# Column and row groups in turn for the small matmuls of the mixers, and y of the RWKV scan kept by chunk with a pair of heads on the partitions

## The chip, the cores and the metric

The kernel runs on one core of a Trainium2 chip. The metric is the time of one execution in device microseconds (us). Everything is fp32; the large products split an operand into a high and a low part and are run as fp32r matmuls, the small ones of the mixers run as fp32.

## What is computed

The reference is one layer of a streaming encoder for 2048 prompt rows and 32 sample rows of 1024 channels. Each row is normalised, projected (`W_in`), sent through four mixers of 256 output channels each, projected back (`W_out`) and added to the residual; a gated feed-forward part follows. The change touches two mixers, B (the RWKV scan) and D (attention). Cut to that:

```
# mixer B, 4 heads of 64; lat_w, lat_a are 32 wide, lat_g is 64 wide
w_log  = -softplus(-(w0 + tanh(lat_w) @ w2)) - 0.5
a_rate = sigmoid(a0 + lat_a @ a2)
gate   = sigmoid(lat_g) @ g2
for each row t, each head:                      # wkv7_step
    sa = S @ a_t
    S  = S * w_t + sa b_t^T + v_t k_t^T
    y  = S @ r_t
y = (y - mean(y)) * rsqrt(var(y) + GN_EPS)      # over the 64 values of a head
y = (y * gn_g + gn_b + bonus) * gate
# mixer D: 4 query heads, 2 key/value heads, window of 128 rows back, whole chunks of 64
p = softmax(q k^T with mask and sink);  o = p v
```

## The kernel before

Three stages follow one another: the mixers with both projections (0 to about 1110 us), the feed-forward gate and up products, and the down projection. In the mixers the prompt runs in eight blocks of 256 rows, each of two tiles of 128 rows, and the sample rows go along with one of the blocks. The code of a block is written as steps named by the letters of `ORD` (L67): scan, projection, attention and so on of this block, the input projection of the next one and the output projection of the one before. A scheduler then orders all instructions of an engine by priorities (a `high_priority` offset on some steps) and by when it thinks an operand is there, so PE's row of small matmuls is filled up with matmuls of the projections (`pj`, `pjd` for the input, `po` for the output, all in `mm3`, L93 to L95). PE executes its row strictly in that order.

PSUM has 8 banks: three for the projections ("mm"), one "nx", two "rk" for the scan and its preparation, two "at" for attention and the low-rank products. The tiles of a tag take turns in its banks; a new tile waits until every reader of the old one is done.

The names in what follows:

- **Scan** (`scan`, in `rwkv`): a tile of 128 rows is worked in two chunks of 64 rows. A chunk computes `wp` from the state `stp` and `aup` (L884), adds a part that is ready (`ww`, L886), makes the state's update `pp` (L891) and the new state on VectorE (L895), and the output `yp`. Of `yp`, rows 64c to 64c+63 are the chunk's 64 rows, and its columns are (pair of heads, head of the pair, value). So all matmuls of a chunk's `yp` write the same 64 PSUM partitions: the state's part `stp`,`arp` (L897, all 128 rows of the array, 64 columns), then per head `wwp`,`trp` (L901) and `vtokp`,`krp` (L902), 64 rows by 64 columns. Which 64 columns of the array a matmul takes follows from the PSUM partitions it writes; which 64 rows, from the partitions that it reads. `pp` writes its two heads of a pair to different 64 partitions, one after the other.
- **Statistics**: once per tile, on all 128 rows: four `bn_stats` and `bn_aggr` (L908, L909), a reciprocal square root (`rsqrt`: a VectorE instruction L117 and a power on GpSimd L118, tile `grsp`), one VectorE instruction for the shift (L911), four ScalarE instructions that write the normalised y, `gynp` (L913). `rwkv_out` transposes `gynp` by pair of heads (L1001) and applies the channel's scale and shift.
- **Attention** (`attn`): for each key/value head `kv` two score matmuls `asp` (L675) that read partitions 64kv to 64kv+63, the softmax, transposes `aptp` into `apt` (L710, L711), and two matmuls `aot` (L713; one in the first tile) that write partitions 64kv to 64kv+63, from the previous and this tile's values `avt`. `apt` has one buffer, so the second head's copy waits for the first head's `aot`.
- **Low-rank products** (`rwkv_prep`, L741): `pw`, `pa`, `pg`, two matmuls each, reading partitions 0 to 31, 32 to 63, 64 to 127 of `lap`; all in the "at" banks.
- **Weights**: in the first block `load_unit` reads `W_in` tile by tile into `wraw` (SyncE, L390), ScalarE makes the high part (L380) and GpSimd, or VectorE for a few, the low part (L382) of `whl`, which is also stored for the later blocks. `wraw` and the residual tiles `xr` of the output projection (L1084) share `XRB` = 6 buffers of 128x256.

Of the kernel before, what the change touches and what calls it, by code (L numbers as in the profile page):

```python
# [8 lines left out]
F32 = mybir.dt.float32  # L9
# [11 lines left out]
GN_EPS = 64e-5  # L21
# [11 lines left out]
def layer(tc, ins, outs):  # L33
# [13 lines left out]
    NB = SEQ // TB  # L47
    SB = 1 if NB > 1 else 0
    ctx = ExitStack()
    XRB = 6  # L50
    PWP = 3000
    RSD = 1
    EVP = 3000
# [594 lines left out]
    def attn(sg, b, i, r, yh, yl):  # L648
        n, PT = sg.name, sg.PT
        samp = sg is seg_s  # L650
        qkv, qn = r["qkv"][i], r["qns"][i]
        gi = b * seg_p.NT + i
        st = b4.tile([128, 12], F32, tag="ast2", name="ast2", bufs=1)
        tp = px([128, 3, 128], "atp", "at")
        for g in range(2):
            TE.transpose(tp[:, g, :PT], qn[:PT, 2 * g:2 * g + 2, :].rearrange("p h d -> p (h d)"), ident[:PT, :PT])
        TE.transpose(tp[:, 2, :PT], qn[:PT, 4:6, :].rearrange("p h d -> p (h d)"), ident[:PT, :PT])
        qt = b4.tile([128, 2, 128], F32, tag="aqt", name="aqt", bufs=1)
        S.activation(qt[:, :, :PT], tp[:, 0:2, :PT], AF.Copy, scale=gq8[:, 0:1])
        if samp:  # L660
            ktr, k0, c0, NK = kt_s, 128, 0, 128 + PT
        else:
            if i == 0:
                if gi:
                    S.activation(ktb[:, 0:128], ktb[:, TB:TB + 128], AF.Copy)
            ktr, k0 = ktb, 128 + i * 128
            c0 = k0 - 128 if gi else k0
            NK = k0 + 128 - c0
        V.tensor_scalar(ktr[:, k0:k0 + PT], tp[:, 2, :PT], P("gk"), None, op0=MUL)
        pr = b4.tile([128, 4, 256], F32, tag="apr", name="apr", bufs=1)  # L670
        for kv in range(2):
            sp = px([128, 2, 256], "asp", "at")
            o = slice(64 * kv, 64 * kv + 64)
            for g in range(2):
                TE.matmul(sp[:PT, g, :NK], qt[o, g, :PT], ktr[o, c0:c0 + NK], start=True, stop=True)  # L675
            if samp:
                V.tensor_copy(pr[:PT, 2 * kv:2 * kv + 2, :NK], sp[:PT, :, :NK])
            else:
                V.tensor_tensor(pr[:PT, 2 * kv:2 * kv + 2, :NK].rearrange("p g (a k) -> p g a k", k=64),
                                sp[:PT, :, :NK].rearrange("p g (a k) -> p g a k", k=64),  # L680
                                amask[:, 4 - NK // 64:].unsqueeze(1).unsqueeze(3).to_broadcast([128, 2, NK // 64, 64]), op=ADD)
        V.tensor_reduce(st[:PT, 0:4], pr[:PT, :, :NK], axis=AX.X, op=MAX)
        V.tensor_tensor(st[:PT, 0:4], st[:PT, 0:4], sinks[:PT], op=MAX)
        V.tensor_tensor(st[:PT, 4:8], sinks[:PT], st[:PT, 0:4], op=SUB)
        V.tensor_scalar(st[:PT, 0:4], st[:PT, 0:4], -1.0, None, op0=MUL)
        sm = b4.tile([128, 8], F32, tag="asm", name="asm", bufs=1)
        S.activation(sm[:PT, 4:8], st[:PT, 4:8], AF.Exp)
        for h in range(4):
            S.activation(pr[:PT, h, :NK], pr[:PT, h, :NK], AF.Exp, bias=st[:PT, h:h + 1], accum_out=sm[:PT, h:h + 1])
        V.tensor_tensor(st[:PT, 8:12], sm[:PT, 0:4], sm[:PT, 4:8], op=ADD)  # L690
        V.reciprocal(st[:PT, 8:12], st[:PT, 8:12])
        for h in range(4):
            S.activation(pr[:PT, h, :NK], pr[:PT, h, :NK], AF.Copy, scale=st[:PT, 8 + h:9 + h])
        if samp:
            vcur = qkv
            parts = [(0, 128, lambda kv: vc_s[:, kv, :]), (128, PT, lambda kv: vcur[:PT, 384 + 64 * kv:448 + 64 * kv])]
        else:
            vt = r["vts"][i]
            parts = [(NK - 128, 128, lambda kv: vt[:, 64 * kv:64 * kv + 64])]
            if NK == 256:  # L700
                vp = vprev[0]
                parts = [(0, 128, lambda kv: vp[:, 64 * kv:64 * kv + 64])] + parts
            vprev[0] = vt
        ot = px([128, 2, 128], "aot", "at")
        for kv in range(2):
            tpp = px([128, 2, 2, 128], "aptp", "at")
            pt = b4.tile([128, 2, 2, 128], F32, tag="apt", name="apt", bufs=1)
            for j, (k0, kn, vf) in enumerate(parts):
                for g in range(2):
                    TE.transpose(tpp[:kn, j, g, :PT], pr[:PT, 2 * kv + g, k0:k0 + kn], ident[:PT, :PT])  # L710
                S.activation(pt[:kn, j, :, :PT], tpp[:kn, j, :, :PT], AF.Copy)  # L711
            for j, (k0, kn, vf) in enumerate(parts):
                TE.matmul(ot[64 * kv:64 * kv + 64, :, :PT], vf(kv), pt[:kn, j, :, :PT], start=j == 0, stop=j == len(parts) - 1)  # L713
        cs = slice(i * 128, i * 128 + PT)
        h = yh[:, :, cs]
        S.activation(h, ot[:, :, :PT], AF.Copy)
        V.tensor_tensor(yl[:, :, cs], ot[:, :, :PT], h.bitcast(F32), op=SUB)
# [6 lines left out]
    def rwkv_prep(sg, r):  # L724
# [10 lines left out]
        lw = tl([128, 2, NC, L + 1], LWT)  # L735
        G.memset(lw[:, :, :, 0:1], 0.0)
        tw, ta, gate = tl([128, 2, T], "t1"), tl([128, 2, T], "t3"), tl([128, 2, T], "gate", GB)
        for nm, o in (("pw", slice(0, 32)), ("pa", slice(32, 64)), ("pg", slice(64, 128))):
            ps = px([128, 2, T], nm, R1P)
            for hp in range(2):  # L740
                TE.matmul(ps[:, hp, :], lw2[o, hp * 128:hp * 128 + 128], lat[o], start=True, stop=True)  # L741
            if nm == "pg":
                S.activation(gate, ps, AF.Copy)
                continue
            for hp in range(2):
                S.activation((tw if nm == "pw" else ta)[:, hp, :], ps[:, hp, :], AF.Tanh, scale=0.5,
                             bias=(hw0 if nm == "pw" else ha0)[:, hp:hp + 1])
# [106 lines left out]
    def rwkv(sg, b, r, last):  # L854
# [16 lines left out]
        def scan(i):  # L871
            tr, kr, kk_, bk_, vt, gg, gt = vs[i]
            wp = px([128, 2, 128], "wp", "rk")
            ww = tl([128, 4, 64], "ww")
            yp = px([128, 2, 128], "yp", "rk")
            for c in range(sg.CPT):
                g = i * sg.CPT + c
                o = slice(c * L, (c + 1) * L)
                s0 = sg.st[sg.si]
                s1 = sg.st[1 - sg.si]  # L880
                sg.si = 1 - sg.si
                sd = tl([128, 2, 128], "sd")
                for hp in range(2):
                    TE.matmul(wp[o, hp, :], gt[:, hp, o], s0[:, hp, :], start=True, stop=True)  # L884
                    S.activation(sd[:, hp, :], s0[:, hp, :], AF.Copy, scale=dd[:, hp, g:g + 1])
                V.tensor_tensor(ww[o], wp[o].rearrange("p a (e v) -> p (a e) v", v=64), gg[o, 1], op=ADD)  # L886
                pp_ = px([128, 2, 64], "pp", "rk")
                for hp in range(2):
                    for src, rhs, st, sp in ((bk_, ww, True, False), (kk_, vt, False, True)):
                        for e in range(2):  # L890
                            TE.matmul(pp_[64 * e:64 * e + 64, hp, :], src[o, 2 * hp + e, :], rhs[o, 2 * hp + e, :], start=st, stop=sp)  # L891
                for hp in range(2):
                    for e in range(2):
                        q = slice(64 * e, 64 * e + 64)
                        V.scalar_tensor_tensor(s1[q, hp, q], pp_[q, hp, :], dd[q, hp, g:g + 1], sd[q, hp, q], op0=MUL, op1=ADD)  # L895
                for hp in range(2):
                    TE.matmul(yp[o, hp, :], ar[:, hp, 1, g * L:(g + 1) * L], s0[:, hp, :], start=True, stop=False)  # L897
                    for e in range(2):
                        h = 2 * hp + e
                        w = slice(64 * e, 64 * e + 64)  # L900
                        TE.matmul(yp[o, hp, w], tr[o, h, L:2 * L], ww[o, h, :], start=False, stop=False)  # L901
                        TE.matmul(yp[o, hp, w], kr[o, hp, e, L:2 * L], vt[o, h, :], start=False, stop=e == 1)  # L902
            st = tl([128, 4, 8], "gst", 2)
            rs = tl([128, 8], "grs", 2)
            yn = tl([128, 4, 64], "gyn", 2)
# [90 lines left out]
    def rwkv_out(sg, yns, gate, bonus, yo, yh, yl):  # L996
        PT = sg.PT
        for i, yn in enumerate(yns):
            yt = px([128, 2, 128], "yt", YT)
            for hp in range(2):  # L1000
                TE.transpose(yt[:, hp, :PT], yn[:PT, 2 * hp:2 * hp + 2, :].rearrange("p a b -> p (a b)"), ident[:PT, :PT])  # L1001
            for hp in range(2):
                S.activation(yo[:, hp, i * PT:(i + 1) * PT], yt[:, hp, :PT], AF.Identity, scale=P("gng", hp), bias=P("gnb", hp))
# [396 lines left out]
```

## Time and profile before

| | us |
|---|---|
| time, median of 3 runs (lowest, highest) | 2594.96 (2594.93, 2601.62) |
| time of the profiled execution | 2597.99 |
| its span, first to last instruction | 2596.3 |
| PE busy in the span | 2448.4 |
| first matmul of the feed-forward part starts | 1112.1 |
| mean granted TensorE clock | 0.972 |

The profile is of one execution, and its times are from the start of the span. A busy PE is one with a matmul in it; matmuls overlap in the array, so the time that one takes from the next is the distance of two starts, and the duration of a single record (0.28 us for many) is longer than that. An fp32 matmul leaves two records in the trace, an fp32r matmul and a transpose one. The granted clock is the share of full speed that TensorE's throttle let it run at.

### The profile page before, as it was taken

To read this page: it belongs to the slowest core of one execution; us is meant where nothing else is said; L and a number is where in the kernel's file an instruction comes from. 1 tells how busy PE (TensorE), PEld (TensorE's weight loads), DVE (VectorE), ACT (ScalarE), POOL (GpSimd) and SP (SyncE) were. 2 spreads that over 40 slices of the span, in tenths; PEclk is the share of its full clock that TensorE was granted. 3 is DMA by queue.
4 is the path that set the end of the run, shared out by engine and by line. 5 is a ranking of instruction groups with operands and counts; after the bars stand their busy time and mean duration, and the time that the engine had idled before them with its cause. 6 is when DMAs were issued, how large, how long until landed. Compare 5 with 4: busy or idle time off the path is not lost. (4 is left out here: it accounts for less than half of the span.)

```text
span 2596.3 us, 43755 instructions
## 1 busy us (share of the span) xinstructions
PE 2448.4 (94%) x16433; PEld 2223.5 (86%) x16433; DVE 1714.3 (66%) x3653; ACT 971.8 (37%) x2098; POOL 940.0 (36%) x778
## 2 busy tenths in 40 slices
PE   6799899999999999879999899998999899999999
PEld 5688779888888888779999899998999878877887
DVE  6796959886959688586787867768777432223221
ACT  5445343434343423444434544345444331212110
POOL 5512412201111100277677676676777420001000
PEclk9899899999999999989999999999999999999999
DMA  7745648655756566733333334234333374446451
GB/s 257 262 171 212 238 169 297 233 190 203 275 210 246 206 253 227 277 102 104 116 112 110 91 98 126 88 112 132 103 114 103 102 220 125 126 117 182 126 143 38
DMA packets 348215, 429.37 MB, mean 165 GB/s; under 512 B 24050, under 2 KB 296707, under 8 KB 323427
## 3 DMA queue, kind: packets, MB, share of 16 engines
q1 hardware_dynamic: 336984, 417.43, 49.0%
q10 hardware_dynamic: 11019, 9.15, 1.0%
q8 instruction: 129, 2.11, 0.3%
q14 instruction: 83, 0.68, 0.1%
HBM read 359.44 MB, written 67.18 MB: 164 GB/s over the span
## 5 line engine op out<-in xcount | busy, mean ns | idle before, releaser
L1227 POOL TENSOR_TENSOR wl<-wf,wh 128x512 fp32r<-128x512 f32 x462 | 662.9, 1439 | 246.3 <-PE gu L95 193.8
L93 PE MATMUL gu<-xh,wh 128*128 128x352 f32 (+1 forms) x1848 | 591.4, 325 | 27.3 <-DVE u L1254 19.7
L95 PE MATMUL gu<-xh,wl 128*128 128x352 f32 (+1 forms) x1848 | 600.3, 325 | 4.4 <-POOL wl L1227 4.4
L94 PE MATMUL gu<-xl,wh 128*128 128x352 f32 (+1 forms) x1848 | 598.8, 324 | 3.7 <-DVE xl L1204 3.6
L1226 ACT ACTIVATE wh<-wf 128x512 fp32r<-128x512 f32 x462 | 290.1, 631 | 470.3 <-PE gu L94 381.7
L93 PEld LDWEIGHTS gu<-xh,wh 128*128 128x128 f32 x1848 | 351.3, 191 | 31.4 <-DVE u L1254 17.6
L94 PEld LDWEIGHTS gu<-xl,wh 128*128 128x128 f32 x1848 | 352.6, 191 | 5.6 <-DVE xl L1204 5.6
L95 PEld LDWEIGHTS gu<-xh,wl 128*128 128x128 f32 x1848 | 352.4, 191 | 5.6 <-POOL wl L1227 5.6
L93 PE MATMUL dn<-dw,ah 128*128 128x512 f32 x704 | 278.0, 397 | 15.2 <-ACT dw L1326 11.9
L95 PE MATMUL dn<-dw,ah 128*128 128x512 f32 x704 | 277.2, 394 | 1.4 <-DVE ah L1346 1.4
L94 PE MATMUL dn<-dw,ah 128*128 128x512 f32 x704 | 274.4, 391 | 2.0 <-DVE dw L1327 1.9
L93 PE MATMUL pj<-xh,whl 128*128 128x256 f32 (+1 forms) x832 | 246.7, 298 | 6.8 <-ACT lap L475 4.8
L95 PE MATMUL pj<-xh,whl 128*128 128x256 f32 (+1 forms) x832 | 240.1, 292 | 7.0 <-POOL whl L382 6.9
L94 PE MATMUL pj<-xl,whl 128*128 128x256 f32 (+1 forms) x832 | 241.6, 292 | 0.4 <-DVE xl L144 0.4
L562 DVE SCALAR_TENSOR_TENSOR accp<-gbp,d_cws,accp 128x256 f32<-128x256 f32 x480 | 231.8, 514 | 0.7
L1345 ACT ACTIVATE ah<-af 128x1408 fp32r<-128x1408 f32 (+1 forms) x68 | 86.5, 1320 | 379.5 <-PE dn L95 345.9
L1358 DVE TENSOR_TENSOR xr<-xr,dn 128x512 f32<-128x512 f32 x32 | 22.0, 688 | 306.0 <-PE dn L95 306.0
L93 PEld LDWEIGHTS pj<-xh,whl 128*128 128x128 f32 x832 | 161.1, 194 | 18.8 <-issue 7.6
L93 PEld LDWEIGHTS dn<-dw,ah 128*128 128x128 f32 x704 | 133.3, 190 | 43.2 <-ACT dw L1326 12.2
L95 PEld LDWEIGHTS pj<-xh,whl 128*128 128x128 f32 x832 | 159.5, 193 | 12.3 <-POOL whl L382 7.4
L94 PEld LDWEIGHTS pj<-xl,whl 128*128 128x128 f32 x832 | 160.8, 194 | 4.3 <-issue 2.4
L94 PEld LDWEIGHTS dn<-dw,ah 128*128 128x128 f32 x704 | 133.0, 189 | 32.9 <-DVE dw L1327 2.6
(512 smaller groups left out, 4806.1 us busy)
## 6 DMA issues: line engine op xcount, KB each, us to landing
whl<-wk_i SPq DMA_DIRECT2D x112, 1024.0 KB, 4.8
whl<-wk_o SPq DMA_DIRECT2D x56, 1024.0 KB, 6.0
af<-act_d SPq DMA_DIRECT2D x32, 1408.0 KB, 7.8
wf<-in_ffn_w_gate_dram SPq DMA_DIRECT2D x132, 256.0 KB, 3.0
wf<-in_ffn_w_up_dram SPq DMA_DIRECT2D x132, 256.0 KB, 3.0
wk_i<-whl SPq DMA_DIRECT2D x16, 1024.0 KB, 5.3
act_d<-act SPq DMA_DIRECT2D x44, 352.0 KB, 2.5
draw<-in_ffn_w_down_dram SPq DMA_DIRECT2D x44, 256.0 KB, 3.2
```

The costliest lines, as they stand in the source:

```text
L93: TE.matmul(out, ah, bh, start=first, stop=False, skip_group_check=more)
L94: TE.matmul(out, ah, bl, start=False, stop=False, skip_group_check=more)
L95: TE.matmul(out, al, bh, start=False, stop=last, skip_group_check=more)
L562: V.scalar_tensor_tensor(acc[:, c, :], gb[:, c, j:j + T], cws[c][:, j:j + 1], acc[:, c, :], op0=MUL, op1=ADD)
L1226: S.activation(hi, q[nm], AF.Copy)
L1227: G.tensor_tensor(lo, q[nm], hi.bitcast(F32), op=SUB)
L1345: S.activation(ah[:, fs_, :n], af[:, fs_, :n], AF.Copy)
L1358: V.tensor_tensor(xr, xr, ps, op=ADD)
```

## The change

1. `yp` of a prompt tile becomes one PSUM tile of 128x128 for each chunk, with (pair of heads, row of the chunk) on the partitions and (head of the pair, value) in the columns. Consecutive matmuls alternate between PSUM partitions 0 to 63 and 64 to 127, and so between the array's two column groups. The part that needs `ww` comes last.
2. The statistics are taken per chunk on the 128 partitions: two `bn_stats`, `bn_aggr` and ScalarE instructions for each chunk, as many as before in a tile, but the reciprocal square root (L117, L118 before) and the shift (L911) run twice per tile.
3. `rwkv_out` transposes by chunk, and its two ScalarE instructions read the pair of heads from the columns.
4. `attn` issues the scores with the heads inside, both heads' `asp` at once, and the `aot` matmuls of both heads together after all transposes, alternating heads; `apt` has two buffers.
5. The low-rank matmuls run over the three products inside; `pg` takes the "nx" bank, where `pw` and `pa` stay in "at".
6. `XRB` goes from 6 to 4.

The sample tile keeps the old layout of `yp`.

```diff
@@ -47,7 +47,7 @@
     NB = SEQ // TB
     SB = 1 if NB > 1 else 0
     ctx = ExitStack()
-    XRB = 6
+    XRB = 4
     PWP = 3000
     RSD = 1
     EVP = 3000
@@ -668,11 +668,13 @@
             NK = k0 + 128 - c0
         V.tensor_scalar(ktr[:, k0:k0 + PT], tp[:, 2, :PT], P("gk"), None, op0=MUL)
         pr = b4.tile([128, 4, 256], F32, tag="apr", name="apr", bufs=1)
+        sps = [px([128, 2, 256], "asp", "at") for _ in range(2)]
+        for g in range(2):
+            for kv in range(2):
+                o = slice(64 * kv, 64 * kv + 64)
+                TE.matmul(sps[kv][:PT, g, :NK], qt[o, g, :PT], ktr[o, c0:c0 + NK], start=True, stop=True)
         for kv in range(2):
-            sp = px([128, 2, 256], "asp", "at")
-            o = slice(64 * kv, 64 * kv + 64)
-            for g in range(2):
-                TE.matmul(sp[:PT, g, :NK], qt[o, g, :PT], ktr[o, c0:c0 + NK], start=True, stop=True)
+            sp = sps[kv]
             if samp:
                 V.tensor_copy(pr[:PT, 2 * kv:2 * kv + 2, :NK], sp[:PT, :, :NK])
             else:
@@ -701,16 +703,19 @@
                 vp = vprev[0]
                 parts = [(0, 128, lambda kv: vp[:, 64 * kv:64 * kv + 64])] + parts
             vprev[0] = vt
-        ot = px([128, 2, 128], "aot", "at")
+        pts = []
         for kv in range(2):
             tpp = px([128, 2, 2, 128], "aptp", "at")
-            pt = b4.tile([128, 2, 2, 128], F32, tag="apt", name="apt", bufs=1)
+            pt = b4.tile([128, 2, 2, 128], F32, tag="apt", name="apt", bufs=2)
+            pts.append(pt)
             for j, (k0, kn, vf) in enumerate(parts):
                 for g in range(2):
                     TE.transpose(tpp[:kn, j, g, :PT], pr[:PT, 2 * kv + g, k0:k0 + kn], ident[:PT, :PT])
                 S.activation(pt[:kn, j, :, :PT], tpp[:kn, j, :, :PT], AF.Copy)
-            for j, (k0, kn, vf) in enumerate(parts):
-                TE.matmul(ot[64 * kv:64 * kv + 64, :, :PT], vf(kv), pt[:kn, j, :, :PT], start=j == 0, stop=j == len(parts) - 1)
+        ot = px([128, 2, 128], "aot", "at")
+        for j, (k0, kn, vf) in enumerate(parts):
+            for kv in range(2):
+                TE.matmul(ot[64 * kv:64 * kv + 64, :, :PT], vf(kv), pts[kv][:kn, j, :, :PT], start=j == 0, stop=j == len(parts) - 1)
         cs = slice(i * 128, i * 128 + PT)
         h = yh[:, :, cs]
         S.activation(h, ot[:, :, :PT], AF.Copy)
@@ -735,10 +740,12 @@
         lw = tl([128, 2, NC, L + 1], LWT)
         G.memset(lw[:, :, :, 0:1], 0.0)
         tw, ta, gate = tl([128, 2, T], "t1"), tl([128, 2, T], "t3"), tl([128, 2, T], "gate", GB)
-        for nm, o in (("pw", slice(0, 32)), ("pa", slice(32, 64)), ("pg", slice(64, 128))):
-            ps = px([128, 2, T], nm, R1P)
-            for hp in range(2):
+        low = {nm: (px([128, 2, T], nm, t), o) for nm, t, o in (
+            ("pw", R1P, slice(0, 32)), ("pa", R1P, slice(32, 64)), ("pg", "nx", slice(64, 128)))}
+        for hp in range(2):
+            for ps, o in low.values():
                 TE.matmul(ps[:, hp, :], lw2[o, hp * 128:hp * 128 + 128], lat[o], start=True, stop=True)
+        for nm, (ps, o) in low.items():
             if nm == "pg":
                 S.activation(gate, ps, AF.Copy)
                 continue
@@ -872,7 +879,11 @@
             tr, kr, kk_, bk_, vt, gg, gt = vs[i]
             wp = px([128, 2, 128], "wp", "rk")
             ww = tl([128, 4, 64], "ww")
-            yp = px([128, 2, 128], "yp", "rk")
+            if sg.CPT == 2:
+                yn = tl([128, 4, 64], "gyn", 2)
+                yns.append(yn)
+            else:
+                yp = px([128, 2, 128], "yp", "rk")
             for c in range(sg.CPT):
                 g = i * sg.CPT + c
                 o = slice(c * L, (c + 1) * L)
@@ -893,6 +904,27 @@
                     for e in range(2):
                         q = slice(64 * e, 64 * e + 64)
                         V.scalar_tensor_tensor(s1[q, hp, q], pp_[q, hp, :], dd[q, hp, g:g + 1], sd[q, hp, q], op0=MUL, op1=ADD)
+                if sg.CPT == 2:
+                    yp = px([128, 128], "yp", "rk")
+                    for hp in range(2):
+                        TE.matmul(yp[64 * hp:64 * hp + 64, :], ar[:, hp, 1, g * L:(g + 1) * L], s0[:, hp, :], start=True, stop=False)
+                    for x, y, q in ((kr, vt, 1), (tr, ww, 0)):
+                        for e in range(2):
+                            for hp in range(2):
+                                h = 2 * hp + e
+                                lhs = x[o, hp, e, L:2 * L] if q else x[o, h, L:2 * L]
+                                TE.matmul(yp[64 * hp:64 * hp + 64, 64 * e:64 * e + 64], lhs, y[o, h, :], start=False, stop=not q and e == 1)
+                    st = tl([128, 2, 8], "gst", 2)
+                    rs = tl([128, 4], "grs", 2)
+                    yv = yp.rearrange("p (e v) -> p e v", v=64)
+                    for e in range(2):
+                        V.bn_stats(st[:, e, 0:6], yv[:, e, :])
+                        V.bn_aggr(st[:, e, 6:8], st[:, e, 0:6])
+                    rsqrt(rs[:, 0:2], st[:, :, 7], 1.0, GN_EPS)
+                    V.scalar_tensor_tensor(rs[:, 2:4], st[:, :, 6], -1.0, rs[:, 0:2], op0=MUL, op1=MUL)
+                    for e in range(2):
+                        S.activation(yn[:, 2 * c + e, :], yv[:, e, :], AF.Identity, scale=rs[:, e:e + 1], bias=rs[:, 2 + e:3 + e])
+                    continue
                 for hp in range(2):
                     TE.matmul(yp[o, hp, :], ar[:, hp, 1, g * L:(g + 1) * L], s0[:, hp, :], start=True, stop=False)
                     for e in range(2):
@@ -900,6 +932,8 @@
                         w = slice(64 * e, 64 * e + 64)
                         TE.matmul(yp[o, hp, w], tr[o, h, L:2 * L], ww[o, h, :], start=False, stop=False)
                         TE.matmul(yp[o, hp, w], kr[o, hp, e, L:2 * L], vt[o, h, :], start=False, stop=e == 1)
+            if sg.CPT == 2:
+                return
             st = tl([128, 4, 8], "gst", 2)
             rs = tl([128, 8], "grs", 2)
             yn = tl([128, 4, 64], "gyn", 2)
@@ -997,6 +1031,13 @@
         PT = sg.PT
         for i, yn in enumerate(yns):
             yt = px([128, 2, 128], "yt", YT)
+            if sg.CPT == 2:
+                for c in range(2):
+                    TE.transpose(yt[:, c, :], yn[:, 2 * c:2 * c + 2, :].rearrange("p a b -> p (a b)"), ident)
+                for hp in range(2):
+                    S.activation(yo[:, hp, i * PT:(i + 1) * PT].rearrange("p (c l) -> p c l", c=2), yt[:, :, 64 * hp:64 * hp + 64],
+                                 AF.Identity, scale=P("gng", hp), bias=P("gnb", hp))
+                continue
             for hp in range(2):
                 TE.transpose(yt[:, hp, :PT], yn[:PT, 2 * hp:2 * hp + 2, :].rearrange("p a b -> p (a b)"), ident[:PT, :PT])
             for hp in range(2):
```

How the rows move on PE, in the scan of one tile. Before, from the first of the second chunk's two `wp` on, with the first chunk's `yp` behind it (`stp0` and `stp1` are the state's two copies):

```order
L884 MATMUL wp_11268<-stp0_235,aup_11167 64x128
L897 MATMUL yp_11270<-stp1_237,arp_10196 64x128
L901 MATMUL yp_11270<-wwp_11269,trp_10253 64x64
L902 MATMUL yp_11270<-vtokp_11187,krp_10254 64x64
L901 MATMUL yp_11270<-wwp_11269,trp_10253 64x64
L902 MATMUL yp_11270<-vtokp_11187,krp_10254 64x64
L897 MATMUL yp_11270<-stp1_237,arp_10196 64x128
```

The same place of PE's row after the change, between the second chunk's two `wp` (now L895; the lines of `yp` are L910 and L916):

```order
L895 MATMUL wp_11340<-stp0_235,aup_11239 64x128
L910 MATMUL yp_11362<-stp1_237,arp_10268 64x128 x2
L916 MATMUL yp_11362<-vtokp_11259,krp_10326 64x64 x4
L916 MATMUL yp_11362<-wwp_11341,trp_10325 64x64 x4
L895 MATMUL wp_11340<-stp0_235,aup_11239 64x128
```

Two groups of five (one 128-row matmul and four 64x64 ones), all ten in one column group, have become one group of ten in which neighbours differ in the column group.

On PE in attention, before: each head's `aot` matmul stands by itself between other work (`aptp_10841` and `aptp_10851` are the two heads' transposes):

```order
L710 MATMUL aptp_10841<-ident_61,apr_10815 128x128 x2
L713 MATMUL aot_10840<-apt_10842,avt_10617 64x256
L891 MATMUL pp_11306<-wwp_11269,btokp_11185 64x64 x2
L891 MATMUL pp_11306<-vtokp_11187,ktokp_11169 64x64 x2
L891 MATMUL pp_11306<-wwp_11269,btokp_11185 64x64 x2
```

On PE after the change, one tile's four `aot` matmuls, of both heads and both value tiles (`apt_10857` and `apt_10865` are the heads, `avt_9134` and `avt_10689` the tiles):

```order
L95 MATMUL pj_11091<-xh_9969,whl_11061 128x256
L718 MATMUL aot_10872<-apt_10857,avt_9134 64x256
L718 MATMUL aot_10872<-apt_10865,avt_9134 64x256
L718 MATMUL aot_10872<-apt_10857,avt_10689 64x256
L718 MATMUL aot_10872<-apt_10865,avt_10689 64x256
L656 MATMUL atp_10880<-ident_61,aqn_10682 128x128 x2
```

They stand in one row, heads in turn.

On SyncE at the start, before (`wk_i_343` is the stored first unit of weights):

```order
L171 DMA gmix<-in_norm_mix_g_dram 128x1024
L390 DMA wraw<-in_w_in_dram 128x128 x8
L390 DMA wraw<-in_w_in_dram 128x256 x4
L385 DMA wk_i_343<-whl 1024x1x128
L390 DMA wraw<-in_w_in_dram 128x256 x4
```

And after:

```order
L390 DMA wraw<-in_w_in_dram 128x128 x4
L1201 DMA gcol<-in_norm_ffn_g_dram 128x8x1
L390 DMA wraw<-in_w_in_dram 128x128 x4
L390 DMA wraw<-in_w_in_dram 128x256 x3
L385 DMA wk_i_343<-whl 1024x1x128
L390 DMA wraw<-in_w_in_dram 128x256 x5
```

A load that the feed-forward part needs, `gcol`, now stands behind the fourth weight tile, and the first store of weights one load earlier.

## The prediction

> **What bounds the kernel now.** I read the page's busy times first, then those in stretches of 130 us, then single matmuls on the timeline.
>
> ```profile
> PE 2448.4 (94%) x16433; PEld 2223.5 (86%) x16433; DVE 1714.3 (66%) x3653; ACT 971.8 (37%) x2098; POOL 940.0 (36%) x778
> ```
>
> PE is busy 94% of the span, the next engine, VectorE, 66%. But the change touches only the mixers, up to about 1110 us, so their stretches count (stretch, its length, busy us and instructions of PE, PEld, VectorE, ScalarE, GpSimd, then granted clock, DMA share, GB/s):
>
> ```profile
> 0.00:130.00 130.00, 90.16 (x738) 81.50 (x738) 88.25 (x301) 60.43 (x167) 68.00 (x96) 0.92 0.76 259
> 130.00:260.00 130.00, 127.69 (x1046) 113.89 (x1046) 107.96 (x350) 59.79 (x179) 22.82 (x28) 0.95 0.53 191
> 260.00:390.00 130.00, 115.52 (x954) 98.32 (x949) 97.21 (x285) 51.81 (x156) 40.54 (x49) 0.91 0.57 203
> 390.00:520.00 130.00, 126.90 (x1044) 115.56 (x1043) 117.86 (x404) 54.43 (x151) 29.14 (x31) 0.96 0.74 266
> 520.00:650.00 130.00, 128.35 (x1136) 112.93 (x1136) 95.68 (x310) 49.67 (x139) 16.73 (x16) 1.00 0.56 197
> 650.00:780.00 130.00, 124.67 (x1058) 112.02 (x1056) 97.86 (x301) 51.45 (x141) 18.96 (x21) 0.97 0.66 243
> 780.00:910.00 130.00, 127.62 (x1076) 112.88 (x1076) 99.70 (x320) 50.91 (x139) 19.72 (x19) 0.99 0.62 224
> 910.00:1040.00 130.00, 125.97 (x1090) 113.03 (x1088) 111.29 (x345) 42.51 (x116) 12.42 (x11) 0.99 0.66 238
> ```
>
> Each is about one of the eight blocks. In four (from 130, 520, 650, 780 us) PE is busy 124.67 to 128.35 of 130 and VectorE 95.68 to 107.96: PE is the bound, and time taken from it is time gained. From 0 us PE is busy 90.16, from 260 us 115.52, so other things end there too; from 390 and 910 us PE is full, but VectorE, at 117.86 and 111.29, would soon be next. The mean granted clock of the eight is 0.96.
>
> **The change part by part.** Prices are distances from start to start in PE's row.
>
> The scan's output `yp`, one chunk of before (start, us, instruction; an x2 is the two records of one fp32 matmul):
>
> ```profile
> 373.17 0.33 PE L891 MATMUL pp<-wwp,btokp 64*64 64x64 f32 x4
> ...
> 373.69 0.28 PE L901 MATMUL yp<-wwp,trp 64*64 64x64 f32 x2
> ...
> 374.04 0.28 PE L902 MATMUL yp<-vtokp,krp 64*64 64x64 f32 x2
> 374.25 0.43 PE L897 MATMUL yp<-stp,arp 128*64 128x128 f32 x2
> 374.61 0.33 PE L901 MATMUL yp<-wwp,trp 64*64 64x64 f32 x2
> ...
> 375.21 0.39 PE L95 MATMUL pj<-xh,whl 128*128 128x256 f32 x1
> ```
>
> `pp` already alternates column groups: its 8 matmuls take 373.69 - 373.17 = 0.52 us. The 8 matmuls of `yp` of the same shape stay in one group and take 0.56 us (to 374.25) for the first four and 0.60 (374.61 to 375.21) for the last: twice as long each. L897 takes 374.61 - 374.25 = 0.36. A chunk's `yp` is two halves of 0.36 + 0.60 = 0.96 us. If they run side by side, as `pp` does, one goes: 32 chunks by 0.96 = 30.7 us. For the 128-row matmul, side by side shows where `wp` (columns 64 to 127) and `yp` (columns 0 to 63) happened to be neighbours:
>
> ```profile
> 368.11 0.32 PE L884 MATMUL wp<-stp,aup 128*64 128x128 f32 x1
> 368.12 0.32 PE L897 MATMUL yp<-stp,arp 128*64 128x128 f32 x1
> 368.27 0.27 PE L884 MATMUL wp<-stp,aup 128*64 128x128 f32 x1
> ```
>
> Two records start 0.01 us apart, the next pair 0.16 later. That takes something back: in 12 to 20 places the order of before has such a mixed pair, and the lone `wp` now pays for itself, 0.32 us (two steps of 0.16): 4 to 6, I take 5. **Term: -26 us.**
>
> The attention's `aot`, alone before:
>
> ```profile
> 506.12 0.65 PE L713 MATMUL aot<-apt,avt 128*64 128x256 f32 x2
> 506.70 0.44 PE L656 MATMUL atp<-ident,aqn 128*128 128x128 f32 x2
> ```
>
> That is 0.58 us each; 62 on the prompt tiles, nearly all by themselves, are 36 us. After, the order has 25 places: 15 with two pairs, 10 with one pair or a single one. A change between the array's full and half shape costs 0.09: 374.04 to 374.25 is 0.21 for a matmul whose neighbours take 0.12. So a first pair costs 0.58, a second behind it 0.58 - 2 x 0.09 = 0.40: 15 x 0.98 + 10 x 0.58 = 20.5, which is -15; and the other work around 37 places fewer loses its own delayed start, taken as one 0.09 each: -3. **Term: -18 us.**
>
> The scores `asp` and the low-rank matmuls:
>
> ```profile
> 343.04 1.14 PE L675 MATMUL asp<-ktb,aqt 64*128 64x256 f32 x8
> 344.11 0.39 PE L93 MATMUL pjd<-whl,xh 128*128 128x256 f32 x1
> ...
> 151.86 1.13 PE L741 MATMUL pw<-lap,lw 32*128 32x256 f32 x4
> 152.92 0.40 PE L93 MATMUL pj<-xh,whl 128*128 128x288 f32 x1
> ...
> 251.54 0.48 PE L741 MATMUL pw<-lap,lw 32*128 32x256 f32 x1
> 251.55 0.48 PE L741 MATMUL pa<-lap,lw 32*128 32x256 f32 x1
> ...
> 252.61 0.39 PE L93 MATMUL pj<-xh,whl 128*128 128x256 f32 x1
> ```
>
> Eight records of `asp` take 1.07 us; four of `pw` alone take 1.06. So the row groups of `asp` already run side by side: nothing to gain. `pw` with `pa` takes 252.61 - 251.54 = 1.07, no more than `pw` alone. At most one visit of about 1 us per block could go, 8 us; the order shows 21 places against 22 before, so I take the near end, **-2 us**.
>
> Sum on PE: -26 - 18 - 2 = -46 us, at the granted 0.96 -48, or 6 us a block. The four blocks where PE is the bound get all, 24; in the other four I count half, since VectorE or the first stretch's loads are next: 12. Realised: -36 us.
>
> The statistics:
>
> ```profile
> L117 DVE TENSOR_SCALAR grsp<-gstp x16: 145/162/171, 124.2 to 1052.7; 128x4 f32<-128x4 f32 x16
> L118 POOL TENSOR_TENSOR grsp<-grsp,nhalf x16: 1006/1018/1976, 124.5 to 1052.9; 128x4 f32<-128x4 f32 x16
> L911 DVE SCALAR_TENSOR_TENSOR grsp<-gstp,grsp x16: 146/157/809, 126.1 to 1054.6; 128x4 f32<-128x4 f32 x16
> ```
>
> A second run per tile adds 16 x (0.162 + 0.157) = 5.1 us to VectorE and 16 x 1.018 = 16 to GpSimd. GpSimd, at most 41 of 130 busy behind the first block, hides its part. VectorE's hides where PE is the bound; of the rest, half counts: **+1 us**, bounds 0 and 5. The transposes and ScalarE instructions keep their number.
>
> The weight buffers, 6 to 4:
>
> ```profile
> L380 ACT ACTIVATE whl<-wraw x104: 309/411/459, 7.8 to 316.0; 128x256 fp32r<-128x256 f32 x96, 128x128 fp32r<-128x128 f32 x8
> L382 POOL TENSOR_TENSOR whl<-wraw,whl x98: 448/737/1702, 9.2 to 318.6; 128x256 fp32r<-128x256 f32 x92, 128x128 fp32r<-128x128 f32 x6
> L390 SPq DMA_DIRECT2D wraw<-in_w_in_dram x72: 327/382/1250, 2.2 to 104.7; - x72
> ...
> wraw<-in_w_in_dram SPq DMA_DIRECT2D x64, 128.0 KB, 3.7
> ...
> SPq L390 <- POOL whl L382: 47.3, 34, 7.5
> ...
> PE pj L95 <- POOL whl L382: 6.9, 1, 6.9
> ```
>
> A buffer's round trip is issue 0.38, landing 3.7, ScalarE 0.41, GpSimd 0.74: 5.2 us. Six buffers allow a tile every 0.87 us, four every 1.31; one came every (104.7 - 2.2)/72 = 1.42. The mean still fits, barely, and SyncE already stood 47.3 us for a buffer. Behind a waiting L390, its queue holds the next weight tiles and the stores of finished units, which no other stage needs soon. PE's wait for what comes of it was 6.9 us; bounds 0 and a doubling. I take **+3 us**, nearer to 0 because the mean fits.
>
> Sum: -36 + 1 + 3 = -32 us. From the profiled execution's 2598 that is 2566; it was 3 us above the median, so **2563 us**.
>
> One rule of the Trainium skill speaks against the change: "TensorE: Matmul & The Clock Gate", Part 3, "The mechanism", says that loading weights overlaps with matmuls in flight only when the row group differs; those of `yp` and `aot` differ in the column group alone, so by it most of the 44 us would not come. The rows of `pp` and of `wp` with `yp` do not agree with it.
>
> **The rivals.**
>
> All of PE's gain comes out and the weights cost nothing: -48 + 1, **2548 us**. For it: VectorE leaves room even at 117.86 of 130. Against: PE idles 40 us of the first stretch.
>
> VectorE and the weights take more: half of everything, -24, and 7 us at the start: **2578 us**. For it: VectorE's 88 to 118 us a block and SyncE's 47.3.
>
> The change doesn't do what it says: matmuls in two column groups do not run side by side in these shapes. Then `yp` saves one shape change a chunk (3 us), `aot` its 3 and the low-rank 2; +4 for the rest: -4, **2591 us**. No row speaks for it; `pp` and `wp` with `yp` speak against it.
>
> Slower: the statistics hold the scan's banks. Both chunks of a tile now have a `yp`, and its bank comes free only when the last L913 has read it:
>
> ```profile
> L902 PE MATMUL yp<-vtokp,krp x8: 218/218/218, 672.2 to 673.5; 64*64 64x64 f32 x8
> L913 ACT ACTIVATE gynp<-yp,grsp x4: 410/421/429, 682.0 to 682.9; 128x64 f32<-128x64 f32 x4
> ```
>
> From the last `yp` to its last reader are 9.4 us. The next `wp` or `pp` waits for a bank, and all of PE's row behind it. If PE stands a third of that in each tile, 16 x 3.1 = 50 us come on top, -32 + 50: **2613 us**. It decides from 2 us a tile (no gain), 2.5 make it slower by more than 0.3%. Against it: one bank waits like this before the change, too, the order has projections behind `yp` as before, and the first chunk's bank has the second chunk's time to come free.
>
> **How the numbers follow.** Forecast 2563: 0.55. All, 2548 or better: 0.20. Half, 2578: 0.14. No overlap, 2591: 0.05. Slower, 2613: 0.06. A measurement tells 0.3%, 7.8 us, from no change, so faster is below 2587. Faster: the first three, but for 0.02 of the half case: 0.87. Same: that and the fourth, 0.07. Slower: 0.06. The range goes from the all-gain case with the low-rank's other 6 us and 2 us more of `yp` (2540) to the half case with the 7 us at the start doubled (2585).
>
> **What would show each step.** `yp`: ten matmuls in about 1.0 us, records in pairs 0.01 us apart. `aot`: the same, four matmuls in 1.0 us. PE's busy time in the mixers down by some 45 us, the first feed-forward matmul at about 1080 us in place of 1112, the later stages as long as before. Weights: PE's wait for `whl` at 10 us or so. Statistics: no wait of PE for L913 over a few us. I am wrong if the pairs start one after the other, if PE's waits for VectorE or L913 rise by what its busy time falls, or if the first stretch loses over 10 us.

## The result and the profile after

| | before, us | after, us |
|---|---|---|
| median of the runs (lowest, highest) | 2594.94 (2585.8, 2601.62) | 2553.84 (2549.38, 2562.36) |
| time of the profiled execution | 2597.99 | 2553.33 |
| its span | 2596.3 | 2551.6 |
| first matmul of the feed-forward part | 1112.1 | 1070.7 |

The ratio is 0.984, 95% interval 0.981 to 0.9871: 41 us less (33 to 49). A second measurement gave 0.9823 (0.9801 to 0.9844). The forecast was 2563, range 2540 to 2585.

The page of the changed kernel, busy times by engine:

```profile
PE 2405.1 (94%) x16433; PEld 2200.6 (86%) x16433; DVE 1716.1 (67%) x3685; ACT 971.4 (38%) x2098; POOL 946.5 (37%) x794
```

PE has as many matmuls as before and 43.3 us less busy time. Where it went shows in the busy times of the two stretches before and behind the first feed-forward matmul; first before the change, then after (columns as in the stretches above):

```profile
0.00:1112.10 1112.10, 1029.61 (x8594) 912.59 (x8594) 853.65 (x2701) 453.04 (x1266) 243.23 (x287) 0.96 0.64 230
1112.10:2596.30 1484.20, 1418.83 (x7841) 1310.87 (x7840) 860.63 (x953) 518.76 (x834) 696.75 (x492) 0.98 0.40 117
```

```profile
0.00:1070.70 1070.70, 985.35 (x8593) 887.34 (x8593) 858.33 (x2734) 455.11 (x1271) 256.25 (x305) 0.96 0.67 239
1070.70:2551.60 1480.90, 1419.80 (x7841) 1313.24 (x7840) 857.80 (x953) 516.32 (x829) 690.28 (x490) 0.98 0.40 117
```

The mixers lose 41.4 us of time and 44.3 us of PE's busy time; idle time of PE there goes from 82.5 to 85.4. The later stages are as before within 3.3 us. VectorE and GpSimd do a little more in less time. So the gain is PE's own work, and its waits as a whole grew by only 2.9 us.

One chunk's `yp` and one tile's `aot` on PE's timeline of the changed kernel (start, us, instruction; records of one line next to each other are one row):

```profile
628.87 0.44 PE L910 MATMUL yp<-stp,arp 128*64 128x128 f32 x4
629.24 0.45 PE L916 MATMUL yp<-vtokp,krp 64*64 64x64 f32 x8
629.52 0.40 PE L916 MATMUL yp<-wwp,trp 64*64 64x64 f32 x8
629.85 0.43 PE L895 MATMUL wp<-stp,aup 128*64 128x128 f32 x2
...
613.47 1.08 PE L718 MATMUL aot<-apt,avt 128*64 128x256 f32 x8
614.49 0.44 PE L656 MATMUL atp<-ident,aqn 128*128 128x128 f32 x2
```

The twenty records of `yp` take 629.85 - 628.87 = 0.98 us, against two halves of 0.96 before. The eight of `aot` take 1.02 us.

The next table sums PE's row over the mixers: for each matmul the distance to the next one's start, cut at 0.7 us so that long waits stay out, added up by output. It is worked out from the trace's records. All distances together are the time from the first matmul on, so that the sum and the cut-off part follow the mixers' time is no finding; the table shows where in PE's row the time went.

| PE's row, us | before | after | difference |
|---|---|---|---|
| `yp` | 65.0 | 35.3 | -29.7 |
| `aot` | 38.1 | 20.0 | -18.1 |
| `aptp` | 21.9 | 15.7 | -6.2 |
| `pw` | 6.2 | 2.5 | -3.7 |
| `pj`, `po`, `pjd` | 667.7 | 679.6 | +11.9 |
| everything else | 250.9 | 256.8 | +5.9 |
| sum | 1049.8 | 1009.7 | -40.1 |
| cut off above 0.7 us | 49.3 | 49.3 | 0 |

Part of what the projections take more shows in the single records. PE sits idle between a projection matmul and the next matmul 46 times where it did 32 times, and the small matmuls break the projections into 324 stretches where there were 299; the first matmul of a stretch takes 0.22 us to the next start, the others 0.12.

### The profile page after: what moved, and what is told of

It reads as the page before. It is cut to its first block, busy times and chain, and to the rows that moved or that the text cites. A ratio compares the mean times of both kernels' runs of the same rounds, so it can differ in the third digit from the quotient of the medians.

```text
span 2551.6 us, 43828 instructions
## 1 busy us (share of the span) xinstructions
PE 2405.1 (94%) x16433; PEld 2200.6 (86%) x16433; DVE 1716.1 (67%) x3685; ACT 971.4 (38%) x2098; POOL 946.5 (37%) x794
## 5 line engine op out<-in xcount | busy, mean ns | idle before, releaser
L562 DVE SCALAR_TENSOR_TENSOR accp<-gbp,d_cws,accp 128x256 f32<-128x256 f32 x480 | 225.0, 496 | 0.8
```

The source lines that it names most:

```text
L562: V.scalar_tensor_tensor(acc[:, c, :], gb[:, c, j:j + T], cws[c][:, j:j + 1], acc[:, c, :], op0=MUL, op1=ADD)
```

## The experiments

All ratios are against the kernel before on the same chip, with the 95% interval; 0.01 is 26 us.

**Each part alone.** The change cut along its parts. Parts 1 to 3, `yp` with its statistics and transposes: the diff's places in `scan` and `rwkv_out` on the kernel before, six buffers, nothing else.

> Before with the parts 1 to 3 of the change alone: yp by chunk in two column groups in turn, its statistics per chunk, the transposes to match; six weight buffers, attention and low-rank matmuls as before. Theory (the matmuls side by side are the gain, three quarters of PE's saving reach the end): PE's row loses 27 us for yp, the end 20 less 1 for the statistics, about 2576. If all of PE's saving reaches the end: 2567. Rival (yp's matmuls do not run side by side, the gain is that of attention's fewer places): 2590 to 2595.

Measured: 2575.61 us, 0.9927 (0.99 to 0.9955), 19 us less. In PE's row `yp` went from 65.0 to 36.5 us, but the row's whole sum only from 1049.8 to 1026.0: other matmuls gave 4.7 us back.

Part 4, attention, needs room that only four weight buffers leave:

```diff
-    XRB = 6
+    XRB = 4
...
-            pt = b4.tile([128, 2, 2, 128], F32, tag="apt", name="apt", bufs=1)
+            pt = b4.tile([128, 2, 2, 128], F32, tag="apt", name="apt", bufs=2)
```

and the diff's two places in `attn`.

> Before with part 4 (scores with heads inside, aot of both heads in turn after all transposes, two apt buffers) and the four weight buffers without which the second apt buffer has no room. Theory: PE's row loses 18 us for aot; with three quarters to the end and +3 for the buffers, 2584; with all of it to the end and nothing for the buffers, 2577. Rival (the gain is yp's alone): 2595.

Measured: 2580.35 us, 0.9933 (0.9917 to 0.995), 17 us less.

Four buffers alone (the first two lines of that diff):

> Before with four weight buffers in place of six, nothing else. Theory: +3 us (0 to 7), 2598, with PE's waits for whl in the first 130 us up. Rival 1: the buffers cost nothing, 2595. Rival 2: they cost 10 us or more, and the change gained that much more elsewhere: 2605.

Measured: 2605.56 us, 1.0035 (1.0019 to 1.0051): 9 us more. The tile `wraw` of this kernel (instruction, count, ns min/median/max, first and last start in us) has the last load of `W_in` at 116.7 us, where it was 104.7:

```profile
L390 SPq DMA_DIRECT2D wraw<-in_w_in_dram x72: 327/328/1110, 2.2 to 116.7; - x72
```

In its waits, SyncE stands 54.7 us for a buffer, 46 times:

```profile
SPq L390 <- POOL whl L382: 54.7, 46, 11.0
```

And on its timeline the second block's first `pw` starts 8.7 us after the 151.86 of before:

```profile
160.55 1.12 PE L741 MATMUL pw<-lap,lw 32*128 32x256 f32 x4
```

So attention's part by itself is 17 + 9 = 26 us, more than the `aot` of the forecast: in PE's row, against four buffers alone, `aot` loses 15.9 us, `aptp` 5.3 and `pw` 3.2.

Part 5 alone, the low-rank matmuls:

```diff
-        for nm, o in (("pw", slice(0, 32)), ("pa", slice(32, 64)), ("pg", slice(64, 128))):
-            ps = px([128, 2, T], nm, R1P)
-            for hp in range(2):
+        low = {nm: (px([128, 2, T], nm, t), o) for nm, t, o in (
+            ("pw", R1P, slice(0, 32)), ("pa", R1P, slice(32, 64)), ("pg", "nx", slice(64, 128)))}
+        for hp in range(2):
+            for ps, o in low.values():
```

> Before with part 5 alone: pw, pa, pg with the products inside, pg in the bank nx. Theory: -2 us, 2593 (0 to -8). Rival: pg's bank nx makes other work wait, up to 5 us slower, 2600.

Measured: 2594.1 us, 0.9995 (0.9983 to 1.0007): nothing that can be told from no change.

Together: with four buffers as the base, `yp` (from the last experiment below, 0.9943) is 0.9943 - 1.0035, 24 us, attention 26, low-rank 1, less the buffers' 9: 42 us, which is what the whole change gave (41, and 46 in the second measurement).

**Is it the turn?** The whole change on one chip, beside versions of it in which the rows are not in turn.

> The whole change beside the three below, on their chip: 2554 by its earlier runs.

Measured: 2552.44 us, 0.9823 (0.9801 to 0.9844).

`yp`, one column group after the other, each with its own 128-row matmul first:

```diff
                     for hp in range(2):
                         TE.matmul(yp[64 * hp:64 * hp + 64, :], ar[:, hp, 1, g * L:(g + 1) * L], s0[:, hp, :], start=True, stop=False)
-                    for x, y, q in ((kr, vt, 1), (tr, ww, 0)):
-                        for e in range(2):
-                            for hp in range(2):
+                        for x, y, q in ((kr, vt, 1), (tr, ww, 0)):
+                            for e in range(2):
```

> The whole change, but the ten matmuls of a chunk's yp one column group after the other (pair of heads outermost): same layout, same statistics, same number of matmuls. Theory (side by side is the gain): PE's row gains back 27 to 30 us; the end 20 (three quarters) to 30 (all) later than the whole change, 2574 to 2584. Rival (the layout or the order of the other work is the gain): within 5 us of the whole change, 2554.

Measured: 2583.1 us, 0.9942 (0.992 to 0.9963): 31 us more than the whole change, and the intervals are apart. A chunk is back at two halves:

```profile
602.77 0.43 PE L910 MATMUL yp<-stp,arp 128*64 128x128 f32 x2
603.13 0.44 PE L915 MATMUL yp<-vtokp,krp 64*64 64x64 f32 x4
603.42 0.39 PE L915 MATMUL yp<-wwp,trp 64*64 64x64 f32 x4
603.74 0.43 PE L910 MATMUL yp<-stp,arp 128*64 128x128 f32 x2
604.10 0.44 PE L915 MATMUL yp<-vtokp,krp 64*64 64x64 f32 x4
604.38 0.39 PE L915 MATMUL yp<-wwp,trp 64*64 64x64 f32 x4
604.71 0.39 PE L95 MATMUL pjd<-whl,xl 128*128 128x256 f32 x1
```

604.71 - 602.77 = 1.94 us, and `yp` in PE's row is 65.4 us, 30.1 more. Layout and statistics are those of the change, and what is left of its gain, 15 us, is no more than attention's part with four buffers gave (17): within the intervals, the gain of `yp` is its order alone. Here 30 us of `yp` in PE's row cost 31 us of time.

`aot`, one head after the other within its place:

```diff
-        for j, (k0, kn, vf) in enumerate(parts):
-            for kv in range(2):
+        for kv in range(2):
+            for j, (k0, kn, vf) in enumerate(parts):
```

> The whole change, but the aot matmuls one head after the other within their place: as few places, no alternation. Theory: 15 places of four matmuls lose 0.8 us each and some of the others 0.4, 14 us of PE's row; the end 10 to 14 later, 2564 to 2568. Rival (the gain of aot is only that its places are fewer): 2554.

Measured: 2553.69 us, 0.9834 (0.9811 to 0.9858), the same as the whole change. That fits the rival's time, but not the whole of its reason; the timeline of this kernel has the place:

```profile
609.84 1.09 PE L718 MATMUL aot<-apt,avt 128*64 128x256 f32 x8
610.87 0.44 PE L656 MATMUL atp<-ident,aqn 128*128 128x128 f32 x2
```

Eight records in 1.03 us, as in turn. The single records of this place start at 0, 14, 267, 281, 483, 497, 699 and 713 ns: in pairs, although in PE's row of the compiled program all of one head's records stand ahead of the other's. PE put them side by side by itself. Then why did it not for `yp`? There the shape changes between the groups (the second group begins with a 128-row matmul). That was tried:

```diff
                         TE.matmul(yp[64 * hp:64 * hp + 64, :], ar[:, hp, 1, g * L:(g + 1) * L], s0[:, hp, :], start=True, stop=False)
-                    for x, y, q in ((kr, vt, 1), (tr, ww, 0)):
-                        for e in range(2):
-                            for hp in range(2):
+                    for hp in range(2):
+                        for x, y, q in ((kr, vt, 1), (tr, ww, 0)):
+                            for e in range(2):
```

> The whole change, but in a chunk's yp the two 128-row matmuls stand first, then the four 64x64 matmuls of one column group, then the four of the other. The run with aot one head after the other cost nothing, and its trace showed the two heads' records side by side although the row has them one after the other. Theory A (PE itself starts a later matmul of the other column group beside an earlier one, as long as the shape doesn't change between them): yp takes as long as in turn, 35 us of PE's row, time as the whole change, 2553. Theory B (neighbours in the row must differ in the column group): the eight 64x64 matmuls take twice as long, 32 x 0.5 = 16 us of PE's row more, 2568.

Measured: 2564.47 us, 0.9872 (0.9854 to 0.9889): 13 us more than the whole change's 0.9823, which was measured on another chip, and `yp` takes 44.0 us of PE's row, 8.7 more. Neither theory as written; the timeline shows what lies between them:

```profile
648.15 0.44 PE L910 MATMUL yp<-stp,arp 128*64 128x128 f32 x4
648.52 0.44 PE L916 MATMUL yp<-vtokp,krp 64*64 64x64 f32 x4
648.80 0.22 PE L916 MATMUL yp<-wwp,trp 64*64 64x64 f32 x1
648.80 0.27 PE L916 MATMUL yp<-vtokp,krp 64*64 64x64 f32 x1
648.86 0.22 PE L916 MATMUL yp<-wwp,trp 64*64 64x64 f32 x1
648.91 0.22 PE L916 MATMUL yp<-vtokp,krp 64*64 64x64 f32 x1
...
649.09 0.39 PE L916 MATMUL yp<-wwp,trp 64*64 64x64 f32 x4
649.41 0.43 PE L895 MATMUL wp<-stp,aup 128*64 128x128 f32 x2
```

The first group's four `vtokp` records run alone. At 648.80 the second group's first `vtokp` record starts beside the first group's first `wwp`, the record that stands four places ahead of it in PE's row, and so before three records that the row has first. Four records of each group run side by side, and the second group's last four run alone. 649.41 - 648.15 = 1.26 us, between 0.98 in turn and 1.94 apart. All 27 chunks whose 20 records stand unbroken in this trace have this order, while in the compiled program all eight records of the first group stand ahead of the second's. So the order is PE's own: within one shape it started a record beside one of the other column group up to four places ahead. It does not execute its row strictly in order, as the part on the kernel before has it. Four records make up one head's half of an `aot` place, so `aot` needs no turn; `yp`, with eight records to a group, does.

**The statistics.** The reciprocal square root twice per chunk:

```diff
-                    rsqrt(rs[:, 0:2], st[:, :, 7], 1.0, GN_EPS)
+                    rsqrt(rs[:, 2:4], st[:, :, 7], 1.0, GN_EPS)
+                    V.scalar_tensor_tensor(rs[:, 0:2], rs[:, 2:4], 0.0, st[:, :, 7], op0=MUL, op1=ADD)
+                    rsqrt(rs[:, 0:2], rs[:, 0:2], 1.0, GN_EPS)
```

> The whole change with the reciprocal square root of each chunk's statistics run a second time behind the first (its result is the same): 32 trips through VectorE, GpSimd and VectorE more, where the change added 16, and the bank of yp held longer by one trip. Theory (the statistics lie beside PE's work): +2 to +4 us, 2556 to 2558. Rival (the banks that the statistics hold are waited for): 3 us a tile, +48, 2602.

Measured: 2549.41 us, 0.982 (0.9793 to 0.9848), no later than the whole change. The theory's 2 to 4 us can't be told from nothing in this interval; the rival's 48 lie far outside it. PE's longest wait for the last reader of `yp` is 2.8 us in the changed kernel and 5.2 here, once each (columns: us in total, times, longest):

```profile
PE wp L895 <- ACT gynp L926: 2.8, 1, 2.8
```

```profile
PE wp L895 <- ACT gynp L928: 5.2, 1, 5.2
```

**The weight buffers within the whole change.** If the transposed probabilities overwrite the ones they come from, `apt` goes and there is room for six or eight buffers:

```diff
-    XRB = 4
+    XRB = 6
...
-            pt = b4.tile([128, 2, 2, 128], F32, tag="apt", name="apt", bufs=2)
-            pts.append(pt)
...
-                S.activation(pt[:kn, j, :, :PT], tpp[:kn, j, :, :PT], AF.Copy)
+                S.activation(pr[:kn, 2 * kv:2 * kv + 2, k0:k0 + PT], tpp[:kn, j, :, :PT], AF.Copy)
...
-                TE.matmul(ot[64 * kv:64 * kv + 64, :, :PT], vf(kv), pts[kv][:kn, j, :, :PT], start=j == 0, stop=j == len(parts) - 1)
+                TE.matmul(ot[64 * kv:64 * kv + 64, :, :PT], vf(kv), pr[:kn, 2 * kv:2 * kv + 2, k0:k0 + PT], start=j == 0, stop=j == len(parts) - 1)
```

> The whole change with the transposed probabilities written over the probabilities that they come from (tile apr) in place of apt: the room of both apt buffers comes free and XRB is 6 again. If the four buffers still cost the whole change what they cost alone (9 us): 2544. If the whole change hides them (its second block starts at 152 us, as before the change, where four buffers alone start it at 161): 2553. Rival: apr is now held until aot has read it, and attention waits: 2560 or more.

> As the one before with XRB 8, in the room that is left. If weight buffers bound the first block: 3 us or so faster than six, 2541. If six suffice (a round trip of 5.2 us over six buffers is 0.87 us a tile against 1.42 needed): as six.

Measured: 2557.7 us, 0.9834 (0.9812 to 0.9857), with six; 2555.57 us, 0.9839 (0.9821 to 0.9856), with eight. Neither beats the change, although the last load of `W_in` starts at 105.5 us with six and at 97.5 with eight. The rival isn't seen either: neither trace shows a wait of a new `apr` for `aot`. The change's own loads of weights end at 111.1 us, later than before:

```profile
L390 SPq DMA_DIRECT2D wraw<-in_w_in_dram x72: 327/328/1906, 2.2 to 111.1; - x72
```

But on its timeline the second block starts no later:

```profile
151.72 0.69 PE L747 MATMUL pw<-lap,lw 32*128 32x256 f32 x2
```

What hides the loss was asked of one more kernel, parts 1 to 3 with four buffers:

> Before with parts 1 to 3 (yp, its statistics, the transposes) and the four weight buffers; attention and low-rank matmuls as before. Four buffers alone cost 9 us and start the second block at 161 us, with attention's part at 159, but the whole change starts it at 152. Theory A (the new yp with its statistics hides the buffers' loss): the second block starts at 152 and the time is that of yp alone, 2578. Theory B (the low-rank matmuls' new order does): it starts at 160 and the time is yp's plus 9, 2587.

Measured: 2585.94 us, 0.9943 (0.9925 to 0.9961), the second block at 157.87:

```profile
157.87 0.48 PE L741 MATMUL pw<-lap,lw 32*128 32x256 f32 x1
```

The second block's start is nearer to theory B, that the low-rank matmuls' new order brings it forward. The time decides nothing: by the ratios it is 4 us more than with parts 1 to 3 and six buffers (0.9943 against 0.9927), in the middle between the theories' 0 and 9, and the two intervals overlap. The new order was not tried with four buffers alone, and the sums above, in which the 9 us are still in the whole, say the opposite of the runs with six and eight. What the four buffers cost inside the whole change stays open between 0 and 9 us.

## Why the prediction was right, and where its terms were off

- **`yp`, -26 us: right in cause, 4 small.** 0.98 us a chunk was forecast as "ten matmuls in about 1.0". The 5 us taken back for a lone `wp` did not come: `wp` is 20.0 us in PE's row before and 20.4 after.
- **`aot`, -18 us: near in size, wrong in what brings it.** The forecast has -15 for `aot` itself and -3 for the work around it; `aot` itself lost 18.1 us of PE's row (20.0 after, where 20.5 was counted, but 38.1 before, where 36 was). The turn is not needed; that both heads' matmuls stand together is. "A first pair costs 0.58, a second behind it 0.40" came out as 1.02 for both.
- **A term was missing:** `aptp` loses 6.2 us of PE's row. It stands in as many places as before (71 before, 72 after), but an `aot` follows 3 of its records where it followed 33. A record with `aot` behind it takes 0.22 us to the next start, one with a projection behind it 0.08 to 0.09.
- **`asp` and the low-rank matmuls, -2 us:** right within what can be measured (-1, with -4 to +2). The 3.7 us that `pw` loses in PE's row are not part 5's doing: `pw` loses 3.2 with attention's part and nothing with part 5 alone (7.0 us for 6.2).
- **"In the other four I count half": this step failed.** The step takes 12 of 48 us off because VectorE or the first stretch's loads would be waited for instead. PE's busy time in the mixers fell by 44.3 us, close to the forecast's "some 45", and 41.4 of them came out as time: PE's idle time rose by 2.9 us, not by 12. VectorE did not become the bound. It is busy 858.33 of 1070.70 us, 80%, and PE's waits for it in the mixers fell from 39.6 to 33.8 us; its waits for loads rose from 15.5 to 26.3 us. `yp` by its order alone says the same: not in turn it was 30 us of PE's row for 31 of time, grouped 9 for 13. Only `yp` without the other parts gave less, 28.5 us of its row for 19 (12 to 26) of time; there, too, the other matmuls take 4.7 us more.
- **PE's sum, -48:** in PE's row the moved matmuls, with `aptp`, lost more than was forecast, 57.7 us, but the projections around them take 11.9 us more and the other groups 5.9, and 40.1 are left. Waits at 14 more places and 25 more stretches of projections are part of that; why the scheduler's order has them wasn't tried. This error and that of the half have opposite signs, so it is partly luck that the forecast of -32 came within 9 us of the measured 41. At 2554 us the kernel is nearer to the rival in which all of PE's gain comes out (2548) than to the forecast (2563).
- **The statistics, +1:** too small to be measured, and cheaper on GpSimd than worked out. The power on two columns takes 0.73 us where that on four took 1.02 (medians); all powers of the scan together, long ones included, take 28.2 us where they took 18.1, 10 more and not 16:

```profile
L118 POOL TENSOR_TENSOR grsp<-grsp,nhalf x32: 688/729/3427, 124.5 to 1017.0; 128x2 f32<-128x2 f32 x32
```

The slower rival, the statistics holding the scan's banks, needed 2 us a tile; the trace has one wait of 2.8 us.
- **The weight buffers, +3:** by themselves 9 (5 to 13), above the 6.9 of the upper bound. "The mean still fits, barely" was the weak point: with four buffers SyncE waits 46 times where it waited 34, and the last tile is asked for 12 us later (116.7 for 104.7). In the whole they cost between 0 and 9.
- **The Trainium skill's rule** ("TensorE: Matmul & The Clock Gate", Part 3, "The mechanism"), by which loading weights overlaps with matmuls in flight only when the row group differs, does not hold for these shapes: pairs that differ in the column group alone start 6 to 7 ns apart in `yp`, and the 31 us of `yp` not in turn hang on it. In the chunk at 629 us the second matmul's weights load from 629.241 us on, while the first one, begun at 629.237, is in flight. The same section of the Trainium skill says that matmuls start strictly in the order of the program; the second group of the grouped `yp`, which starts before three records that stand ahead of it, speaks against that too.

## What to carry to other kernels

Small fp32 matmuls that use half of the array's columns cost about half when neighbours in PE's row use different halves. Put matmuls of one shape together first: here a change of shape cost about 0.1 us (0.15 us from the last 64x64 record of a `yp` to the next start, where one record to the next takes 0.06). Then alternate wherever one half has more than four records in a row. Ask whether the second engine makes the first one wait, not how busy it is: here 41 of the 44 us of PE's busy time came out with VectorE 80% busy. A change in the number of buffers that is made only for room deserves a run of its own; here it took back 9 us by itself.

## What the runs showed of the hardware

- PE starts an fp32 matmul record beside one of the other column group that stands up to four places ahead of it in PE's row, and so before three that the row has first (`yp` grouped, 27 of 27 unbroken chunks; by the starts in pairs also `aot` one head after the other). It does not do so across a change of shape (`yp` with a 128-row matmul between its groups: 1.94 us, nothing side by side).
- 64x64 matmuls of 64 columns take 58 ns a record in one column group (`yp` not in turn) and 58 to 59 ns a pair in two (`yp` in turn): the second of a pair costs nothing.
- GpSimd's power on 128 partitions takes 0.73 us for two columns and 1.02 for four.
